# The four sums of tokens for the FFN's Strassen products by accumulating DMAs, with two quarters of the normed tokens kept negated

## The chip, the core and the metric

The kernel runs on one core of one Trainium2 chip. A core has five engines that run their own queues in order: TensorE (PE) multiplies, VectorE (DVE), ScalarE (ACT) and GpSimd (POOL) work elementwise, and SyncE (SP) issues most DMAs. GpSimd can issue DMAs as well, from its own queue. All DMAs run on the core's 16 DMA engines. The metric is the device time of one execution in microseconds (us), as the median of several runs.

## What is computed

The reference is one step of a two-layer recurrent decoder over 512 prompt tokens and 8 x 8 sample tokens, 576 in all, with 1024 channels. Each layer mixes tokens, adds a projection to `x`, and then applies the feed-forward network (FFN) that the change is about:

```
def _rmsnorm(x, w):
    xf = x.astype(jnp.float32)
    y = xf * lax.rsqrt(jnp.mean(xf * xf, axis=-1, keepdims=True) + NORM_EPS)
    return (y * w.astype(jnp.float32)).astype(x.dtype)
...
    x = x + y.astype(x.dtype)
    h = _rmsnorm(x, lw['ffn_norm'])
    g, u = jnp.split(h @ lw['w_ffn_in'], 2, axis=-1)
    x = x + ((jax.nn.silu(g) * u) @ lw['w_ffn_out']).astype(x.dtype)
```

`g` and `u` have 2816 columns each, which the kernel takes as 22 column blocks of 128.

## The kernel before

Channels lie on the 128 partitions: `x[k]` is a tile of 128 channels by 576 tokens, k from 0 to 7, and a *half* is 288 tokens. Every product in half precision is made of three matmuls: an fp32 operand is split into a high part (a cast, on ScalarE) and a low part (what the cast lost, on VectorE or GpSimd), and hi x hi, hi x lo and lo x hi are added up in PSUM.

`out_proj` adds the mixer's projection to `x`, sums squares for the norm, and starts the norm of half 0 (`norm_half` with `keep`). `norm_tiles` writes the normed value over `x[k]`, casts it to the high part of `h[k]` on ScalarE (L464) and makes the low part (L465) on VectorE, for some k on GpSimd.

`ffn` then works off the first three of the 22 blocks as plain GEMMs, `up(m, w, half)`: blocks 0 to 2 of half 0, then blocks 0 to 2 of half 1. Each fills two PSUM buffers (`fb`) of a ring of four; they come free when `gated` has read them with `fsg` on ScalarE and `fy` on VectorE. While they run, the norm of half 1 is made, and `strassen_tokens` makes four sums of quarters of the normed tokens. A quarter is four channel tiles of one half: b11 (k 0 to 3, half 0), b12 (k 0 to 3, half 1), b21 (k 4 to 7, half 0) and b22 (k 4 to 7, half 1). The sums overwrite the quarters, and `split` makes the 32 parts `st0` to `st3` of them.

Blocks 3 to 21 use Strassen's scheme in Winograd's form: 7 products instead of 8 for a 2 x 2 arrangement of (g, u) x (half 0, half 1). `strassen_weights` prepares the weights' seven operands of a block (`hA..`, `hS..`) with one accumulating DMA (L1709), three GpSimd additions (L1707) and seven splits on ScalarE (L1703) and VectorE (L1704). The preparation of block m+1 runs beside the products of block m. The order on each engine's queue is written out by a scheduler when the kernel is built; at run time each queue is worked off strictly in that order, and an operation that waits for a semaphore holds back all behind it.

Of the kernel before, what the change touches and what calls it, by code (L numbers as in the profile page):

```python
# [10 lines left out]
F32 = mybir.dt.float32  # L11
F16 = mybir.dt.float16
I32 = mybir.dt.int32
AF = mybir.ActivationFunctionType
ALU = mybir.AluOpType
PSUM = bass.MemoryType.PSUM
ADD, SUB, MUL, MAX, MIN = ALU.add, ALU.subtract, ALU.mult, ALU.max, ALU.min
# [6 lines left out]
DEPTH = 2  # L24
DFF = 2816
KT = D // 128
# [24 lines left out]
PBASE = {}  # L51
# [123 lines left out]
class Net:  # L175
# [159 lines left out]
    def setup(self):  # L335

        nc, t, cp = self.nc, self.io, self.cp
        rows = self.wp.tile([128, GW], F32, tag="raw", name="prow")[:, :128]
        for n, k in PARAMS:
            b = PBASE[n][0]  # L340
# [14 lines left out]
        for i, a in enumerate(self.x0):  # L355
            k, hs = 2 * (i % 4), slice(HW * (i // 4), HW * (i // 4) + HW)
# [13 lines left out]
        nc.tensor.transpose(ps, rows[:NPAR, :], self.ident[:NPAR, :NPAR])  # L370
        nc.vector.tensor_copy(self.pc[:, 2 * KT:], ps[:, 2 * KT:])
        nc.vector.tensor_scalar(self.pc[:, 2 * KT:4 * KT], self.pc[:, 2 * KT:4 * KT], HS, None, op0=MUL)
        for n in ("rw_w0", "rw_a0"):
            b, k = PBASE[n]
            nc.vector.tensor_scalar(self.pc[:, b:b + 2 * k], self.pc[:, b:b + 2 * k], 0.5, None, op0=MUL)
        b = PBASE["rw_kk"][0]
        nc.vector.tensor_scalar(self.pc[:, b:b + 4], self.pc[:, b:b + 4], 2.0 ** 15, None, op0=MUL)
        b = PBASE["rw_ka"][0]
# [3 lines left out]
        b = PBASE["hg_lb_logits"][0]  # L382
# [74 lines left out]
    def norm_tiles(self, name, l, half, r, x, keep):  # L457
        nc = self.nc
        hs = slice(half * HW, half * HW + HW)
        for k in range(KT):  # L460
            o = x[k] if keep else self.t("e", [128, HW], "nrm")
            hi, lo = self.h[k][:, 0, hs], self.h[k][:, 1, hs]
            nc.vector.scalar_tensor_tensor(o, x[k], self.par(name, l, k), r, op0=MUL, op1=MUL)
            nc.scalar.copy(hi, o)  # L464
            (nc.gpsimd if k % 3 == 2 or l == half == 0 and k % 2 else nc.vector).tensor_tensor(lo, o, hi, op=SUB)  # L465
# [1157 lines left out]
    def mix(self, l, prepared):  # L1623
# [3 lines left out]
        for half in range(2):  # L1627
            for i in range(3):
                for _ in range(2):
                    next(units[i])  # L1630
                if half == 0 and i == 0:
                    if l:
                        self.norm_half("attn_norm_w", l, 1)
                    else:
                        self.first_norm(1)
                        setup = self.setup()
                        next(setup)
                if l == 0 and half == 1 and i == 0:
                    run(setup)
# [37 lines left out]
    def strassen_tokens(self):  # L1677

        nc = self.nc
        out = [self.t("gd", [128, 4, 2, HW], f"st{i}", F16) for i in range(4)]  # L1680
        h0, h1 = slice(0, HW), slice(HW, T)
        src = []
        for k in range(4):
            b11, b12, b21, b22 = (self.x[k + o][:, h] for o in (0, 4) for h in (h0, h1))
            for i, (dst, a, b) in enumerate(((b11, b12, b11), (b12, b22, b12), (b22, b22, b11), (b21, b21, b22))):
                nc.gpsimd.tensor_tensor(dst, a, b, op=SUB)
                src.append(((0, 2, 1, 3)[i], k, dst))
        yield out
        for i in (3, 1, 0, 2):
            for j, k, dst in src:  # L1690
                if i == j:
                    self.split(out[i][:, k, 0], out[i][:, k, 1], dst)
            yield out

    def strassen_weights(self, key, load, ring, **rings):
# [258 lines left out]
```

## Time and profile before

| what | value |
|---|---|
| median of 3 runs | 2200.59 us (2200.28 to 2201.81) |
| the profiled execution | 2207.72 us |
| its span, first to last instruction | 2205.9 us |
| TensorE, VectorE, ScalarE, GpSimd busy | 92%, 74%, 49%, 31% |
| mean granted TensorE clock | 0.977 of full speed |
| sums of tokens, layer 0 | from 735.50 us |
| first Strassen matmul, layer 0 | 765.84 us |

Times in the rows are in us from the start of the span, unless marked ns. In a timeline each row has its start, its length (for several operations merged into a row, from the first's start to the last's end), the engine, the source line, the operation, `written<-read`, the shape and the count; in brackets stands how long the engine idled before it, and for whom. In the rows by line, the busy time and the mean length in ns follow the first bar. The rows of a window have its length, then for each engine the busy time and the number of instructions in the order TensorE, its weight loads, VectorE, ScalarE, GpSimd, and then the granted clock, the busy share of the DMA engines and GB/s.

### The profile page before, as it was taken

How to read it: one execution, taken by the hardware profiler on the slowest of the kernel's cores; microseconds unless marked ns; L12 is line 12 of the kernel's file. 1: busy time of each engine (PE TensorE's matmuls, PEld its weight loads, DVE VectorE, ACT ScalarE, POOL GpSimd, SP SyncE). 2: the span in 40 equal slices, each digit the busy share in tenths (PEclk: the TensorE clock that was granted, in tenths of full speed). 3: DMA queues.
4: the chain of work that ended last, by engine and by line, in shares of the span. 5: the costliest groups of instructions: out<-in, count | busy, mean ns of one | idle time of the engine just before them, and what ended most of it. 6: DMA issues, size and time to landing. Idle time of an engine off the chain costs nothing.

```text
span 2205.9 us, 42236 instructions
## 1 busy us (share of the span) xinstructions
PE 2039.1 (92%) x15754; PEld 1612.3 (73%) x15754; DVE 1636.6 (74%) x3409; ACT 1081.3 (49%) x2524; POOL 682.3 (31%) x889
## 2 busy tenths in 40 slices
PE   7989999998888899999999889989998988999998
PEld 5767787786676677777777778768776766777776
DVE  7889667768785899863488986586788779998441
ACT  6554546345444555442466355453645465554332
POOL 2223222146550544320012142213465316443000
PEclk9999999999999999999999999999999999999999
DMA  6312224333435344343421222242343443443331
GB/s 181 84 41 62 58 58 110 77 83 92 116 98 177 80 116 120 87 135 103 122 68 46 58 62 60 73 111 62 87 120 88 131 141 97 111 116 87 121 106 51
DMA packets 373498, 209.59 MB, mean 95 GB/s; under 512 B 59810, under 2 KB 360410, under 8 KB 373292
## 3 DMA queue, kind: packets, MB, share of 16 engines
q1 hardware_dynamic: 365516, 192.73, 31.6%
q0 software_dynamic: 7776, 14.16, 3.6%
q8 instruction: 124, 2.03, 0.4%
q14 instruction: 82, 0.67, 0.1%
HBM read 173.72 MB, written 16.59 MB: 86 GB/s over the span
## 4 chain that ended last, share of the span: by engine, by line
PE 47%; DVE 28%; ACT 8%; issue 7%; DMA 5%; POOL 3%; SPq 1%; DVEq 0%; ACTq 0%; POOLq 0%
PE pb L243 5%; PE pb L242 5%; PE pb L241 5%; PE xb L243 4%; PE xb L242 4%; PE xb L241 4%; DVE hA L1704 4%; DVE hS L1704 3%; DVE sc L1745 2%; DVE fy L1776 2%; DVE whl L229 2%; DVE su L1745 2%; PE fsS L1731 2%; PE fsS L1729 2%; PE fsS L1730 2%
## 5 line engine op out<-in xcount | busy, mean ns | idle before, releaser
L241 PE MATMUL pb<-h,whl 128*128 128x288 f16 (+1 forms) x1504 | 435.8, 290 | 4.4 <-ACT h L464 2.2
L243 PE MATMUL pb<-h,whl 128*128 128x288 f16 (+1 forms) x1504 | 435.5, 290 | 3.2 <-DVE whl L229 3.1
L242 PE MATMUL pb<-h,whl 128*128 128x288 f16 (+1 forms) x1504 | 436.0, 290 | 0.6 <-DVE h L465 0.4
L229 DVE SCALAR_TENSOR_TENSOR whl<-raw,whl 128x512 f16<-128x512 f32 (+1 forms) x352 | 253.8, 730 | 134.3 <-ACT whl L228 132.2
L242 PEld LDWEIGHTS <-whl 128*128 128x128 f16 (+1 forms) x2784 | 275.4, 99 | 88.0 <-issue 13.5
L243 PEld LDWEIGHTS <-whl 128*128 128x128 f16 (+1 forms) x2784 | 275.1, 99 | 88.0 <-issue 12.7
L241 PEld LDWEIGHTS <-whl 128*128 128x128 f16 (+1 forms) x2784 | 277.2, 100 | 76.6 <-issue 3.6
L228 ACT ACTIVATE whl<-raw 128x512 f16<-128x512 f32 (+1 forms) x352 | 213.3, 618 | 168.2 <-PE pb L243 51.9
L243 PE MATMUL xb<-fa,whl 128*128 128x288 f16 x704 | 201.3, 286 | 0.0
L242 PE MATMUL xb<-fa,whl 128*128 128x288 f16 x704 | 201.3, 286 | 0.0
L241 PE MATMUL xb<-fa,whl 128*128 128x288 f16 x704 | 201.3, 286 | 0.0
L1729 PE MATMUL fsA<-h,hA 128*128 128x288 f16 x432 | 124.3, 288 | 14.9 <-DVE gu L1550 10.8
L1729 PE MATMUL fsS<-st,hS 128*128 128x288 f16 x456 | 132.6, 291 | 5.9 <-ACT hS L1703 5.9
L1731 PE MATMUL fsS<-st,hS 128*128 128x288 f16 x456 | 132.4, 290 | 0.4 <-DVE hS L1704 0.3
L1730 PE MATMUL fsS<-st,hS 128*128 128x288 f16 x456 | 132.5, 291 | 0.0
L1731 PE MATMUL fsA<-h,hA 128*128 128x288 f16 x432 | 124.2, 288 | 1.7 <-DVE hA L1704 1.6
L1730 PE MATMUL fsA<-h,hA 128*128 128x288 f16 x432 | 124.3, 288 | 0.0
L1707 POOL TENSOR_TENSOR raw<-raw 128x512 f32<-128x512 f32 x52 | 79.0, 1520 | 134.2 <-DVE hA L1704 129.7
L1729 PEld LDWEIGHTS <-hS 128*128 128x128 f16 x864 | 85.7, 99 | 35.9 <-ACT hS L1703 13.7
L1704 DVE SCALAR_TENSOR_TENSOR hA<-sraw,hA 128x512 f16<-128x512 f32 x110 | 103.1, 945 | 10.6 <-ACT hA L1703 10.6
L1707 POOL TENSOR_TENSOR sraw<-sraw 128x512 f32<-128x512 f32 x60 | 89.7, 1499 | 51.4 <-DVE hA L1704 45.7
L1731 PEld LDWEIGHTS <-hS 128*128 128x128 f16 x864 | 85.7, 99 | 24.8 <-DVE hS L1704 2.6
(486 smaller groups left out, 5257.8 us busy)
## 6 DMA issues: line engine op xcount, KB each, us to landing
raw<-in_w_in SPq DMA_DIRECT2D x208, 256.0 KB
sraw<-in_w_ffn_in SPq DMA_DIRECT2D x40, 512.0 KB
raw<-in_w_ffn_out SPq DMA_DIRECT2D x80, 256.0 KB
raw<-in_w_ffn_in SPq DMA_DIRECT2D x78, 256.0 KB
x<-xd SPq DMA_DIRECT2D x32, 288.0 KB
raw<-sraw POOLq DMA_DIRECT2D x34, 256.0 KB, 3.3
sraw<-in_w_in SPq DMA_DIRECT2D x32, 256.0 KB
raw<-in_w_out SPq DMA_DIRECT2D x32, 256.0 KB
```

The lines of the kernel that those rows point to most:

```text
L228: nc.scalar.activation(hl[:, 0, :n], raw[:, :n], AF.Copy, scale=WS)
L229: nc.vector.scalar_tensor_tensor(hl[:, 1, :n], raw[:, :n], WS, hl[:, 0, :n], op0=MUL, op1=SUB)
L241: nc.tensor.matmul(ps, wh, hi, start=i == 0, stop=False)
L242: nc.tensor.matmul(ps, wh, lo, start=False, stop=False)
L243: nc.tensor.matmul(ps, wl, hi, start=False, stop=i == len(ks) - 1)
L1704: nc.vector.scalar_tensor_tensor(hl[:, 1], a, WS, hl[:, 0], op0=MUL, op1=SUB)
L1707: nc.gpsimd.tensor_tensor(dst, a, b, op=op)
L1729: nc.tensor.matmul(ps, w[a][:, 0, k], hi, start=k == 0, stop=False)
L1730: nc.tensor.matmul(ps, w[a][:, 0, k], lo, start=False, stop=False)
L1731: nc.tensor.matmul(ps, w[a][:, 1, k], hi, start=False, stop=k == 3)
L1745: nc.vector.tensor_tensor(o, a, p, op=ADD)
L1776: nc.vector.scalar_tensor_tensor(y, u, PH * AS, sg, op0=MUL, op1=MUL)
```

## The change

The 16 subtractions on GpSimd (four sums, four tiles each, 128 x 288 in fp32) become 16 DMAs that GpSimd issues and that add one SBUF tile onto another. [...] Two of the four sums, `st0` and `st3`, come out with the other sign, which `split` turns. GpSimd keeps the low parts of odd k among the quarters that are not negated.

```
@@ setup
+        b, k = PBASE["ffn_norm_w"]
+        self.npc = cp.tile([128, DEPTH * k], F32, name="npc")
+        nc.vector.tensor_scalar(self.npc, self.pc[:, b:b + DEPTH * k], -1.0, None, op0=MUL)
@@ norm_tiles
             hi, lo = self.h[k][:, 0, hs], self.h[k][:, 1, hs]
+            if keep:
+
+                neg = (k < 4) == (half == 1)
+                w = self.npc[:, KT * l + k:KT * l + k + 1] if neg else self.par(name, l, k)
+                nc.vector.scalar_tensor_tensor(o, x[k], w, r, op0=MUL, op1=MUL)
+                nc.scalar.activation(hi, o, AF.Copy, scale=-1.0 if neg else 1.0)
+                if neg:
+                    nc.vector.scalar_tensor_tensor(lo, o, -1.0, hi, op0=MUL, op1=SUB)
+                else:
+                    (nc.gpsimd if k % 2 else nc.vector).tensor_tensor(lo, o, hi, op=SUB)
+                continue
@@ strassen_tokens
-        for k in range(4):
-            b11, b12, b21, b22 = (self.x[k + o][:, h] for o in (0, 4) for h in (h0, h1))
-            for i, (dst, a, b) in enumerate(((b11, b12, b11), (b12, b22, b12), (b22, b22, b11), (b21, b21, b22))):
-                nc.gpsimd.tensor_tensor(dst, a, b, op=SUB)
-                src.append(((0, 2, 1, 3)[i], k, dst))
+        b11, b12, b21, b22 = ([self.x[k + o][:, h] for k in range(4)] for o in (0, 4) for h in (h0, h1))
+
+        for j, dst, a in ((0, b11, b12), (2, b12, b22), (1, b22, b11), (3, b21, b22)):
+            for k in range(4):
+                nc.gpsimd.dma_start(out=dst[k], in_=a[k], accum_op=ADD)
+                src.append((j, k, dst[k]))
         yield out
         for i in (3, 1, 0, 2):
             for j, k, dst in src:
                 if i == j:
-                    self.split(out[i][:, k, 0], out[i][:, k, 1], dst)
+                    self.split(out[i][:, k, 0], out[i][:, k, 1], dst, -1.0 if i in (0, 3) else 1.0)
             yield out
```

Line numbers of the changed kernel are higher by 3 to 15 behind these edits: L465 is now L473 and L475, L1686 is L1701, L1703 is L1718, L1707 is L1722, L1709 is L1724 and L1774 is L1789.

GpSimd's queue in layer 0 from the DMA ahead of the sums on, before (`x0` to `x7` are the tiles of `x`, each named for both halves; `h2` and `h5` are low parts of half 1):

```order
L1709 DMA sraw_9671<-sraw_9671 128x512
L1686 TENSOR_TENSOR x0_8557<-x0_8557 128x288
...
L1686 TENSOR_TENSOR x0_8557<-x4_8843,x0_8557 128x288
L465 TENSOR_TENSOR h2_9099<-x2_8699,h2_9099 128x288
...
L465 TENSOR_TENSOR h5_9102<-x5_8854,h5_9102 128x288
...
L1686 TENSOR_TENSOR x7_8876<-x7_8876,x3_8771 128x288
L1686 TENSOR_TENSOR x7_8876<-x7_8876 128x288
L1709 DMA raw_9338<-sraw_9340 128x512
L1707 TENSOR_TENSOR raw_9334<-raw_9338,raw_9334 128x512
```

And the same stretch of the changed kernel:

```order
L1724 DMA sraw_9673<-sraw_9673 128x512
L1701 DMA x0_8559<-x0_8559 128x288
...
L1701 DMA x1_8629<-x5_8856 128x288
L475 TENSOR_TENSOR h5_9104<-x5_8856,h5_9104 128x288
...
L1701 DMA x3_8773<-x7_8878 128x288
L475 TENSOR_TENSOR h7_9106<-x7_8878,h7_9106 128x288
L1701 DMA x4_8845<-x0_8559 128x288
...
L1701 DMA x7_8878<-x7_8878 128x288
L1724 DMA raw_9340<-sraw_9342 128x512
L1722 TENSOR_TENSOR raw_9336<-raw_9340,raw_9336 128x512
```

The sums are now made kind by kind instead of tile by tile, and the `h` parts left to GpSimd are h5, behind six of the DMAs, and h7, behind eight.

ScalarE's queue behind the casts of half 1, before (`fa` is a block's activation, `fsg` its gate read from PSUM, `st` the splits of the sums, `hA11` the first operand of the next weights):

```order
L464 CAST h7_9104<-x7_8876 128x288
L248 ACTIVATE st3_9317<-x4_8843 128x288
L248 ACTIVATE st3_9317<-x5_8854 128x288
L248 ACTIVATE fa1_9392<-fy_9395 128x288
L248 ACTIVATE st3_9317<-x6_8865 128x288
L248 ACTIVATE st1_9315<-x4_8843 128x288
L1774 ACTIVATE fsg_9450<-fb_9399 128x288
L248 ACTIVATE st3_9317<-x7_8876 128x288
...
L1703 ACTIVATE hA11_9757<-raw_9334 128x512
L1774 ACTIVATE fsg_9506<-fb_9456 128x288
```

And in the changed kernel:

```order
L471 ACTIVATE h7_9106<-x7_8878 128x288
L248 ACTIVATE fa1_9394<-fy_9397 128x288
L1789 ACTIVATE fsg_9452<-fb_9401 128x288
L248 ACTIVATE fa2_9451<-fy_9454 128x288
L248 ACTIVATE st3_9319<-x4_8845 128x288
...
L248 ACTIVATE st3_9319<-x7_8878 128x288
L248 ACTIVATE st1_9317<-x6_8867 128x288
L1789 ACTIVATE fsg_9508<-fb_9458 128x288
...
L1718 ACTIVATE hA11_9759<-raw_9336 128x512
L248 ACTIVATE fa0_9280<-fy_9510 128x288
```

The gate and the activations of half 0's blocks 1 and 2 have moved ahead of the splits, and the gate of half 1's block 0 stands behind seven of them; of those, the splits of `st3` wait for the last of the four sums. VectorE's queue has the same turn with `fy` and the low parts.

## Rows read from the trace of the kernel before

**Rows 1.** From the page: busy us, share of span and instructions of TensorE.

```profile
PE 2039.1 (92%) x15754; PEld 1612.3 (73%) x15754; DVE 1636.6 (74%) x3409; ACT 1081.3 (49%) x2524; POOL 682.3 (31%) x889
```

**Rows 2.** Windows: a stretch of the Strassen blocks of layer 0.

```profile
800.00:850.00 50.00, 47.84 (x389) 37.80 (x387) 49.87 (x81) 26.72 (x57) 23.66 (x19) 1.00 0.47 124
```

**Rows 3.** Chain of waits, 733 to 770 us: start, length, what, times.

```profile
740.47 0.91 POOL h L465
...
751.61 0.90 POOL x L1686
752.53 3.57 ACT st L248 x11
...
758.25 0.61 DVE hA L1704
...
765.84 0.28 PE fsA L1729
```

**Rows 4.** Chain of waits, 1815 to 1855 us (layer 1).

```profile
1834.28 0.90 POOL x L1686
```

**Rows 5.** Timeline of GpSimd, 640 to 800 us.

```profile
734.89 0.88 POOL L1709 DMA_DIRECT2D sraw<-sraw  x1 [7.75 <-DVE x L463]
735.50 2.60 POOL L1686 TENSOR_TENSOR x<-x 128x288 f32<-128x288 f32 x3
...
752.44 0.88 POOL L1709 DMA_DIRECT2D raw<-sraw  x1
```

**Rows 6.** Instructions of L463 and L465: ns min/median/max, first and last start.

```profile
L463 DVE SCALAR_TENSOR_TENSOR x<-x,pc,rstd x32: 505/518/3372, 713.5 to 1826.2; 128x288 f32<-128x288 f32 x32
...
L465 DVE TENSOR_TENSOR h<-x,h x21: 444/453/1046, 714.8 to 1828.5; 128x288 f16<-128x288 f32 x21
```

**Rows 7.** Waits of TensorE, 733 to 770 us: total, times, longest.

```profile
PE fb L242 <- DVE h L465: 4.2, 4, 2.6
PE fb L241 <- ACT fsg L1774: 2.1, 1, 2.1
PE fb L241 <- DVE fy L1776: 1.1, 1, 1.1
PE fsA L1729 <- ACT fsg L1774: 0.8, 1, 0.8
```

**Rows 8.** Accumulating DMA: GpSimd by line, two windows, issue with us to landing.

```profile
L1709 POOL DMA_DIRECT2D raw<-sraw x34 | 30.0, 883 | 70.5 <-DVE fy L1776 44.5 <-DVE hA L1704 15.9 <-DVE su L1745 6.7
...
734.90:736.30 1.40, 1.40 (x14) 1.10 (x13) 1.40 (x2) 1.39 (x3) 1.40 (x3) 1.00 0.00 0
736.30:737.80 1.50, 1.50 (x15) 1.20 (x13) 1.50 (x1) 0.51 (x2) 1.50 (x3) 1.00 0.96 175
...
sraw<-sraw POOLq DMA_DIRECT2D x1, 256.0 KB, 3.3
```

**Rows 9.** Loads: SyncE's timeline from 740 us; the page's hardware queue (packets, MB, share).

```profile
743.15 7.12 SPq L1798 DMA_DIRECT2D sraw<-in_w_ffn_in  x4
...
q1 hardware_dynamic: 365516, 192.73, 31.6%
```

**Rows 10.** DMA issues, 1955 to 1968 us: KB each, us to landing.

```profile
sraw<-sraw POOLq DMA_DIRECT2D x1, 256.0 KB, 3.2
raw<-sraw POOLq DMA_DIRECT2D x1, 256.0 KB, 4.9
```

**Rows 11.** Timeline of VectorE, 700 to 800 us.

```profile
713.55 1.38 DVE L463 SCALAR_TENSOR_TENSOR x<-x,pc,rstd 128x288 f32<-128x288 f32 x3 [3.65 <-ACT rstd L445]
...
715.21 3.23 DVE L463 SCALAR_TENSOR_TENSOR x<-x,pc,rstd 128x288 f32<-128x288 f32 x4
...
745.79 0.68 DVE L465 TENSOR_TENSOR h<-x,h 128x288 f16<-128x288 f32 x1
...
753.01 2.67 DVE L250 TENSOR_TENSOR st<-x,st 128x288 f16<-128x288 f32 x7 [0.20 <-ACT st L248]
...
758.17 0.69 DVE L1704 SCALAR_TENSOR_TENSOR hA<-raw,hA 128x512 f16<-128x512 f32 x1
```

## The prediction, made before the changed kernel ran

> **What bounds the kernel now.** I read the page first. TensorE holds 92% of the span [rows 1], so whatever the change touches off TensorE counts only where TensorE, or the engine that feeds it, waits. Next I read the windows of the Strassen blocks: from 800 to 850 us VectorE is busy 49.87 of 50.00 us and TensorE 47.84 [rows 2]. VectorE sets the pace there, so a Strassen stage that starts late ends late by as much, and one that starts early ends early by as much.
>
> Then I asked what releases that stage. The chain of waits around its start runs almost without a break through the work that the change replaces: VectorE's norms, GpSimd's `h` and `x` operations until 751.61 + 0.90, ScalarE's splits of the token sums from 752.53, VectorE's first `hA` of the next weights at 758.25, and TensorE's first Strassen matmul at 765.84 [rows 3]. In layer 1 the last `x` operation starts at 1834.28 [rows 4], 1082.7 us after that of layer 0, and the steps behind it repeat, so I work out layer 0 and double it.
>
> In GpSimd's timeline the sums begin at 735.50, behind a DMA issue at 734.89, with two `h` parts among them; the next DMA issue comes at 752.44 [rows 5]. So 16 subtractions and two `h` parts take 735.50 to 752.51, 17.0 us. Two things besides happen in that time. VectorE's norm multiply, 0.518 us in the median, goes up to 3.372, and its `h` subtraction from 0.453 up to 1.046 [rows 6]: the two engines hold each other up. And TensorE waits 4.2 us for `h`, 2.1 for `fsg` and 1.1 for `fy` [rows 7].
>
> **The change, part by part, for one layer.** The sum's question is when the last token sum is there: 752.51 before; after, when the sixteenth DMA lands.
>
> *Start.* The DMA at 734.89 stays and takes 0.88 us [rows 5, 8]. The first sum's DMA can be issued at 735.77.
>
> *Issue.* GpSimd's cost of one DMA is 0.88 us [rows 8], for 128 rows of 2 KB; ours has 128 rows of 1152 B. The next operation begins 0.61 us after a DMA's start [rows 5], so one issue costs between 0.61 and 0.88. I take 0.84, near the full duration: an operation recorded as started may still wait for the one ahead, and no row shows two such DMAs in a row. The two `h` parts left in the queue (now h5 and h7) cost 0.91 each in the chain [rows 3]; I count 0.85, with less of VectorE in the way. The sixteenth issue then starts at 735.77 + 15 x 0.84 + 2 x 0.85 = 750.1.
>
> *Transfer.* The trace has the accumulating DMA on 256 KB alone. Its engines stand still until 1.4 us after the issue, are 0.96 busy for the next 1.50 (so 1.44 us), and it has landed 3.3 after the issue [rows 8]: 1.45 + 1.44 + 0.36. For 144 KB, 144/256 of 1.44 gives 0.81. The bound from below is the plain hardware queue: 192.73 MB in 31.6% of 2205.9 us is 3.6 us per MB [rows 9], 0.53 us for 147 KB; no row shows an accumulating transfer that fast, so I take 0.83 (rows shorter by half keep their fixed part). The sixteenth lands at 750.1 + 1.45 + 0.83 + 0.36 = 752.7 if nothing else moves.
>
> *Dependencies.* A b12 sum waits until the b11 sum of its tile has landed, a b22 sum for the b12 one, a b21 sum for the b22 one. Four issues lie between a sum and the one that needs it, 4 x 0.84 = 3.4 us against 1.45 + 0.83 + 0.36 = 2.6 to landing. The waits are covered as long as landing stays under 3.4, and not when issues come at 0.61.
>
> *Other transfers.* The same engines load weights: four `sraw` loads are issued between 743.15 and 750.27 [rows 9]. TensorE's progress releases them, so they fall into the sums' time after too. 256 KB is 0.26 x 3.6 = 0.9 us each, 3.7 us in all. The sums alone fill the engines for 16 x 0.83 = 13.3 us from 737.2. That loads do delay an accumulating DMA is seen where they overlap: one lands after 4.9 us instead of 3.2 [rows 10]. With none of the loads in the way the end is 752.7, with all of it 750.5 + 3.7 + 0.36 = 754.6; I count 0.7 of it, and since a delayed landing also delays the issues that wait for it, I take 754.0.
>
> *Behind the last sum.* VectorE has 13 operations left before `hA`, each 0.37 us after the one ahead (7 in 2.67 [rows 11]), 4.8 us; ScalarE's split ahead of the first, one of those that come 11 in 3.57 [rows 3], with its hand-overs is some 0.6. That makes 5.4 us, against 758.17 - 752.51 = 5.7 before [rows 11]. So `hA` starts at 754.0 + 5.4 = 759.4, 1.2 us late. From `hA` on, the GpSimd additions, the `hS` splits and the evacuations that free PSUM for the blocks stand as before. TensorE's last wait of 0.8 ahead of the first block [rows 7] gives back some 0.2, since its other work is then long done. That is +1.0 us a layer.
>
> *What is freed, and why it does not pay.* VectorE's operations return to 0.45 and 0.52 us: about 8 us of its time, between 735 and 747. TensorE's waits for `h`, 4.2 us, shrink to about 2: the h7 part stands in GpSimd's queue behind eight DMAs, at 735.77 + 8 x 0.84 + 0.85 = 743.3, and ends at 744.2, where the last `h` came at 745.79 + 0.68 = 746.47 [rows 11]. The waits of 2.1 and 1.1 go, since `fsg` and `fa` now stand ahead of the splits. TensorE reaches the end of its six GEMMs some 5 us earlier, and waits there, because `fsg` of the next pair stands behind the `hS` that needs GpSimd's addition, which needs `hA`. VectorE idles from about 741 until the first b21 sum lands.
>
> *The rest.* The `npc` multiply (128 x 16, once, in the setup) and ScalarE's cast that becomes an activation of the same shape cost nothing that I count. In layer 0 VectorE takes over three of GpSimd's five `h` parts of the first half, 3 x 0.45 = 1.3 us more. Against it, four norm multiplies there take 3.23 us where three took 1.38 just before [rows 11], 1.4 us over their pace, which GpSimd's five parts caused. The two even out; without that cover the half-1 norms would be 1.3 us late, once.
>
> **Sum.** 2 x 1.0 = +2.0 us. The profiled execution took 2207.72 us (span 2205.9 and 1.8 around it), 7.1 over the median of 2200.59; I add the difference to the median: 2202.6, that is 0.1%. A measurement here tells 0.2% or 4.4 us from no change.
>
> **Pages against rows.** The stretched 3.372 and 1.046 us of VectorE show in the rows that two engines exclude each other [rows 6]. The Trainium skill, SBUF — State Buffer, Who interferes with whom, says that a VectorE instruction with two SBUF inputs contends with a GpSimd instruction that reads SBUF, by a lock held for the whole instruction; by this rule the lock goes away with the change, and the trace agrees so far. If VectorE were the path, the page's rule would give the first rival. The Trainium skill, DMA: Bandwidth & Descriptors, Anatomy of one DMA, puts a DMA at 2.0 us plus bytes over 436 GB/s, 2.3 us for ours as an estimate; by it the sums would be bound by issue alone and the last would land at 752.4, a gain of 0.4 us a layer. The row at 3.3 us for 256 KB, where the page gives 2.6, speaks against it.
>
> **Rivals.**
> *VectorE is the path (faster).* If the splits were not held in queue order behind the last sum, TensorE's 4.2 + 2.1 + 1.1 us a layer [rows 7] would be won: 2200.6 - 14.8 = 2185.8. The order of ScalarE's queue speaks against it. 0.05.
> *The DMAs are quick (faster).* Issue at 0.61, transfer at 0.53, loads in the gaps: the sixteenth issue starts at 747, landing at 749.8, `hA` at 755.2, 2.9 us early, 2194.8. It decides from a landing before 750.8. For it: the 0.61 that the row shows; against it: the engine time of 1.44 us per 256 KB. 0.13.
> *The transfers are the bound (slower).* All 3.7 us of loads, 0.87 a transfer, and landings over 3.4 us that stop GpSimd at its in-order waits: the last lands at 756, `hA` at 761.4, 3.2 late less the 0.2, 2206.6. It decides from a landing after 755.2. For it: 0.96 busy engines and the 4.9 us; against it: most landings alone take 3.2 to 3.3. Behind GpSimd's waiting DMA stand h7, which TensorE waits for, and the next weights' DMA and additions. 0.32 with its tail.
> *No change that can be measured:* the forecast. 0.50.
>
> **The numbers.** Faster by over 0.2% 0.18, within 0.2% 0.50, slower 0.32. The bounds of issue, transfer and loads give landings of 749.5 to 756.5, -6.6 to +7 us; leaving out the first rival and the last of the slow tail, the range is 2195 to 2209.
>
> **What would show it.** Right: 32 DMA issues of `x` near 0.84 us apart on GpSimd; VectorE's norms of the second half at 0.5 us; the last sum landing near 754 and the first `hA` near 759.4; TensorE's wait for `h` halved and a longer wait ahead of the first Strassen matmul. Wrong: issues 0.6 us apart, landings under 2.4 us, or a Strassen stage that no longer starts with this `hA`.

## The result, and the profile after

The changed kernel takes 2214.09 us (median of 4 runs, 2213.85 to 2214.68) against 2201.2 before (4 runs, 2200.28 to 2203.31): ratio 1.006, interval 1.0048 to 1.0072. A second series gave 2217.58 against 2204.58, ratio 1.0056 (1.0044 to 1.0068). It is slower by 12 to 13 us, where the forecast was 2.0 and the range ended at 2209, 8 us above the median of before.

The page of the changed kernel, to be read beside [rows 1] and the queues: TensorE does the same instructions, VectorE is busy for 18 us less, and the software queue's transfers take 5.2% of the span.

```profile
PE 2045.4 (92%) x15754; PEld 1616.8 (73%) x15754; DVE 1618.4 (73%) x3413; ACT 1079.0 (49%) x2524; POOL 679.1 (31%) x886
...
q0 software_dynamic: 12384, 18.88, 5.2%
```

VectorE's timeline of the changed kernel in layer 0. What [rows 6] showed as up to 3.372 us is gone: norms go at 0.5 us, and the longest takes 0.992. Then VectorE stands idle for 13.62 us.

```profile
731.19 1.38 DVE L470 SCALAR_TENSOR_TENSOR x<-x,npc,rstd 128x288 f32<-128x288 f32 x3 [1.30 <-ACT rstd L448]
...
733.28 1.37 DVE L470 SCALAR_TENSOR_TENSOR x<-x,pc,rstd 128x288 f32<-128x288 f32 x3
...
753.22 0.46 DVE L252 SCALAR_TENSOR_TENSOR st<-x,st 128x288 f16<-128x288 f32 x1 [13.62 <-ACT st L248]
```

GpSimd's timeline of the same stretch, which answers to [rows 5]. The sixteen DMAs and two `h` parts run from 734.60 to 751.92 + 0.86 = 752.78, 18.2 us, where sixteen subtractions and two `h` parts took 17.0.

```profile
734.60 3.84 POOL L1701 DMA_DIRECT2D x<-x  x4
739.02 1.75 POOL L1701 DMA_DIRECT2D x<-x  x2 [0.58 <-DVE fy L1791]
...
743.40 1.05 POOL L475 TENSOR_TENSOR h<-x,h 128x288 f16<-128x288 f32 x1
744.08 4.77 POOL L1701 DMA_DIRECT2D x<-x  x5
749.43 1.75 POOL L1701 DMA_DIRECT2D x<-x  x2 [0.58 <-DMA x<-x]
751.92 0.86 POOL L1701 DMA_DIRECT2D x<-x  x1 [0.74 <-DMA x<-x]
752.51 1.16 POOL L1724 DMA_DIRECT2D raw<-sraw  x1
```

The chain of waits of the changed kernel, which answers to [rows 3]. Where VectorE and GpSimd stood, landings now stand (`DMA x<-x`), and the last sum is there at 751.92 + 4.60 = 756.52. From there to the first `hA` of the next weights, 762.12, it is 5.6 us.

```profile
735.67 5.18 DMA x<-x
...
744.67 4.48 DMA x<-x
...
749.43 1.75 POOL x L1701 x2
...
751.92 4.60 DMA x<-x
...
758.44 1.47 DVE st L252 x4
...
762.12 0.61 DVE hA L1719
...
762.86 2.20 POOL raw L1722
...
770.84 0.31 PE fsA L1744
```

The DMA queues of the changed kernel from 732.69 to 757.19, 24.5 us (packets, MB, share of the 16 engines). With 78.6% and 15.7% the engines are all but full from the first sum to the last (one window, 744 to 746 us, has a share of 0.65). The stretch holds the sixteen sums and two DMAs of 256 KB, at 1.44 us each [rows 8]: (0.786 x 24.5 - 2 x 1.44) / 16 = 1.02 us a sum. This is time of packets: from 736.30 to 756.50 us the shares add up to 1.09, so packets overlap on the engines, and spread over them a sum takes some 1.02 / 1.09 = 0.94 us (an estimate). The weights' loads take 0.157 x 24.5 = 3.8 us.

```profile
q0 software_dynamic: 2589, 2.88, 78.6%
q1 hardware_dynamic: 2122, 1.05, 15.7%
```

All instructions of the sums' line in the changed kernel: a DMA lands 4.5 us after its start in the median.

```profile
L1701 POOL DMA_DIRECT2D x<-x x32: 859/1184/2237, 734.6 to 1839.3; - x32
...
DMA to landing us min/median/max: 3.0/4.5/6.0
```

TensorE's waits from 728 to 775 us in the changed kernel, to be read beside [rows 7]. The wait for `h` has not halved (in the profile of the second series it is 3.6), and 5.0 us of waits now stand at the first Strassen products: 1.9 ahead of the first matmul, 3.1 behind its first twelve.

```profile
PE fb L242 <- POOL h L475: 5.3, 2, 3.3
PE fsA L1744 <- DVE fy L1791: 3.1, 1, 3.1
PE fsA L1744 <- ACT fsg L1789: 1.9, 1, 1.9
```

In TensorE's timeline the first Strassen matmul is the one at 766.06; the row of 770.84 in the chain above is the thirteenth.

```profile
766.06 0.28 PE L1744 MATMUL fsA<-h,hA 128*128 128x288 f16 x1 [1.89 <-ACT fsg L1789]
...
770.84 0.31 PE L1744 MATMUL fsA<-h,hA 128*128 128x288 f16 x1 [3.15 <-DVE fy L1791]
```

Where is the time lost? The stage ends with the first matmul of the output GEMM (`xb`). In the kernel before that is 972.89 - 733.45 = 239.44 us behind the first norm of half 1, in the changed one 976.69 - 731.19 = 245.50 (timelines of VectorE and TensorE).

```profile
733.45 1.38 DVE L463 SCALAR_TENSOR_TENSOR x<-x,pc,rstd 128x288 f32<-128x288 f32 x3 [1.30 <-ACT rstd L445]
...
972.89 0.29 PE L241 MATMUL xb<-fa,whl 128*128 128x288 f16 x1
```

```profile
976.69 0.29 PE L241 MATMUL xb<-fa,whl 128*128 128x288 f16 x1
```

The same points read from the traces of these kernels, counted from the first norm of half 1, mean of both layers (and of two profiles for the first two rows), in us:

| kernel | last sum there | first hA | first xb | ratio to before |
|---|---|---|---|---|
| before | 19.1 | 24.7 | 240.2 | 1 |
| changed | 24.5 | 30.0 | 246.0 | 1.0056 |
| 72 KB a sum (e_half) | 21.6 | 27.1 | 243.7 | 1.0050 |
| 18 KB a sum (e_tiny) | 21.2 | 27.0 | 242.9 | 1.0026 |
| no chain (e_nochain) | 23.1 | 25.8 | 241.7 | 1.0027 |
| splits as sums land (e_order) | 24.5 | 16.2 | 242.3 | 1.0018 |
| `h` on VectorE (e_hdve) | 24.2 | 29.0 | 244.7 | 1.0040 |
| GpSimd additions (e_gpadd) | 19.6 | 25.6 | 242.2 | 1.0029 |
| half by DMA, half VectorE (e_mix) | 15.2 | 21.8 | 237.7 | 0.9983 |
| VectorE additions (e_dve) | 12.7 | 21.3 | 236.6 | 0.9976 |
| before, sums on VectorE (b_dve) | 13.1 | 21.1 | 235.0 | 0.9959 |

The change costs 5.8 us a layer in this stage, 11.6 in all, and 5.3 of the 5.8 are there at the first `hA`. The spans of these profiles differ by 10.1 us in the mean (2212.4 and 2218.2 against 2205.9 and 2204.5) and not by 11.6, mostly because in layer 0 the first norm of half 1 comes 1.3 us sooner; the medians differ by 12 to 13.

### The profile page after: what moved, and what is told of

It reads as the page before. It is cut to its first block, busy times and chain, and to the rows that moved or that the text cites. A ratio compares the mean times of both kernels' runs of the same rounds, so it can differ in the third digit from the quotient of the medians.

```text
span 2212.4 us, 42268 instructions
## 1 busy us (share of the span) xinstructions
PE 2045.4 (92%) x15754; PEld 1616.8 (73%) x15754; DVE 1618.4 (73%) x3413; ACT 1079.0 (49%) x2524; POOL 679.1 (31%) x886
## 4 chain that ended last, share of the span: by engine, by line
PE 49%; DVE 29%; issue 7%; ACT 7%; DMA 5%; POOL 2%; SPq 0%; DVEq 0%; POOLq 0%; ACTq 0%
PE pb L243 5%; PE pb L242 5%; PE pb L241 5%; PE xb L243 4%; PE xb L242 4%; PE xb L241 4%; DVE hA L1719 3%; DVE hS L1719 3%; DVE sc L1760 2%; DVE fy L1791 2%; DVE whl L229 2%; DVE su L1760 2%; PE fsS L1746 2%; PE fsS L1744 2%; PE fsS L1745 2%
## 5 line engine op out<-in xcount | busy, mean ns | idle before, releaser
L243 PEld LDWEIGHTS <-whl 128*128 128x128 f16 (+1 forms) x2784 | 275.5, 99 | 86.7 <-issue 11.6
L1744 PE MATMUL fsA<-h,hA 128*128 128x288 f16 x432 | 125.1, 290 | 21.7 <-DVE gu L1564 9.1
L1722 POOL TENSOR_TENSOR raw<-raw 128x512 f32<-128x512 f32 x52 | 79.1, 1521 | 140.2 <-DVE hA L1719 135.7
L1719 DVE SCALAR_TENSOR_TENSOR hA<-sraw,hA 128x512 f16<-128x512 f32 x110 | 99.6, 914 | 11.8 <-ACT hA L1718 11.8
L1722 POOL TENSOR_TENSOR sraw<-sraw 128x512 f32<-128x512 f32 x60 | 90.0, 1504 | 54.2 <-DVE hA L1719 52.4
```

The source lines that it names most:

```text
L243: nc.tensor.matmul(ps, wl, hi, start=False, stop=i == len(ks) - 1)
L1719: nc.vector.scalar_tensor_tensor(hl[:, 1], a, WS, hl[:, 0], op0=MUL, op1=SUB)
L1722: nc.gpsimd.tensor_tensor(dst, a, b, op=op)
L1744: nc.tensor.matmul(ps, w[a][:, 0, k], hi, start=k == 0, stop=False)
```

## The experiments

**The two kernels again.** The kernel before, unchanged:

> The kernel before, unchanged, profiled once more. Its first profile is an execution of 2207.72 us, 6.5 over the median of the others. If that is chance: about 2201 us, and the two traces differ at a few places by 6.5 us together, which tells how much of the 6.3 us between the two profiles belongs to the change and how much more the change costs beside it. If the profiler itself costs 6.5 us for this kernel: about 2207.5 again.

It took 2206.25 us, by this number alone nearer to the second reading. But the 26 runs of before in its series spread from 2197.35 to 2209.64 with a median of 2204.42, and the profiled executions of other kernels lie on either side of their medians (e_dve 2195.95 against 2199.49, e_order 2209.82 against 2209.15). So the first profile, 2207.72, was more likely an execution from the upper part of a spread than the profiler's price. Its stage takes the same: 19.0 to 19.1 to the last sum in both profiles and layers.

> The changed kernel itself, timed beside more runs of the kernel before, whose runs now spread from 2197 to 2210 us with a median of 2204.4. If the 12.9 us are right: 2214 against 2204, ratio 1.004 to 1.006. If the kernel before only had a good series: the changed kernel spreads as widely, and its ratio falls towards the 1.003 that the two profiles show.

2217.58 against 2204.58: the loss stands, and both kernels move by some us from series to series.

**Additions in place of the DMAs**, on GpSimd (e_gpadd) and on VectorE (e_dve). The quarters b12 and b21 are normed with the negated weights `npc` here as in the changed kernel, so that an addition makes the difference:

```
-                nc.gpsimd.dma_start(out=dst[k], in_=a[k], accum_op=ADD)
+                nc.gpsimd.tensor_tensor(dst[k], dst[k], a[k], op=ADD)   # e_gpadd
+                nc.vector.tensor_tensor(dst[k], dst[k], a[k], op=ADD)   # e_dve
```

> Negated norms and signs of the changed kernel, but each sum by a GpSimd addition in place of an accumulating DMA. Theory 'transfers' (the cost is the DMA engines, full from the first sum to the last): the loss goes, 2198 to 2203, with the last sum done at about 15.5 to 17.5 us after the first one starts. Rival 'negation' (VectorE's part of the change costs): stays near 2210 or over.

2211.09, ratio 1.0029 (1.0019 to 1.0039): the time lies where the rival "negation" had it. The last sum is there at 19.6, 17.0 behind the start of the first, as the theory had it; so the DMAs' lateness is gone, but a loss of half the size is not (2.0 of the 5.8 us a layer at `xb`). Its chain of waits points to another cause than the negated norms: the order of the sums puts the last `h` part at 749.16, 16.8 behind the first norm of half 1, and TensorE starts behind it. In the kernel before it stood at 745.79, 12.3 behind. This was not tried by itself, so negation is not ruled out.

```profile
749.16 0.91 POOL h L475
...
750.12 0.40 PE fb L242
```

The additions on GpSimd also bring the stretched norms back, up to 4.475 us where the DMAs left 0.992 and additions on VectorE 0.994. So it is GpSimd's arithmetic that holds VectorE up, as the prediction read [rows 6].

```profile
L470 DVE SCALAR_TENSOR_TENSOR x<-x,pc,rstd x16: 504/518/4475, 712.4 to 1830.0; 128x288 f32<-128x288 f32 x16
```

> As the one with GpSimd additions, but the sixteen additions are VectorE's. VectorE idles 13.6 us behind its norms in the changed kernel. Theory 'transfers': 16 x about 0.45 us, the last sum some 7.5 us behind the last norm, near 747 on the scale of the changed kernel, so the first hA some 6 us earlier than before and 9 earlier than in the changed kernel; GpSimd and VectorE no longer hold each other up: 2201 - 2 x 5 = about 2191. Rival 'the stage is bound elsewhere' (TensorE's GEMMs or fsg ahead of it): within 3 us of before.

2199.49, ratio 0.9976 (0.9966 to 0.9985): 4.9 us under the kernel before of its series, between the two expectations. The sums are there 6 us earlier than before and `hA` 3.4; 3.6 a layer arrive at `xb`. It fell short of the 5 expected: from the last sum to `hA` it is now 8.7 us and not 5.6, with VectorE at the splits, and TensorE waits 5.0 us for `fsg`.

**No sum waits for another**, first try: each DMA adds a constant tile.

```
-                nc.gpsimd.dma_start(out=dst[k], in_=a[k], accum_op=ADD)
+                nc.gpsimd.dma_start(out=dst[k], in_=self.cst[:, :HW], accum_op=ADD)
```

> The sixteen accumulating DMAs as in the changed kernel, but each adds the same constant tile, so that none waits for another sum (the sums are not those of the reference; this prices the chain). Theory 'transfers': the engines stay full, the last one lands within 1 us of 756.5 counted on the changed kernel's scale (22 us behind the first issue), 2211 to 2215 us. Rival 'chain' (GpSimd's queue waits for landings): issues come 0.6 to 0.9 apart without gaps, the last lands 3 to 5 us earlier, 2203 to 2208.

2203.51, ratio 0.9998 (0.9986 to 1.001). The time lies in the rival's range, but it tells nothing apart: with a source that is there from the start, eight of the sixteen DMAs went out before the norms of half 1, so it took away the chain and half of the crowd at once.

**No sum waits for another**, second try, with the constant tile held back until the first norm of half 1:

```
+                if half and not k:
+                    nc.vector.scalar_tensor_tensor(self.cst[:, :1], o[:, :1], 0.0, self.cst[:, :1], op0=MUL, op1=ADD)
```

> The sixteen accumulating DMAs at the place, in the order and of the size of the changed kernel, but each adds one constant tile, which a 128 x 1 operation of VectorE behind the first norm of the second half holds back until then. No sum reads another sum, so the waits for a landing four issues back go (the sums are not the reference's). The changed kernel: 24.5 us from the first norm of the second half to the last landing, hA at 30.0; with an eighth of the bytes 19.5 to 22.9, hA 25.7 to 28.4. Theory 'full engines': the waits only pass on what the engines do anyway, last landing 23 to 25, hA 28.5 to 30.5, ratio 1.004 to 1.006. Rival 'chain': GpSimd issues in 16.0 us without a gap, last landing 21 to 22, hA 26.5 to 27.5, ratio 1.002 to 1.0035.

2209.63, ratio 1.0027 (1.0016 to 1.0039). GpSimd's timeline has no gap: the issues end at 744.10 + 8.61 = 752.71, 16.2 us behind the first one at 736.53.

```profile
736.53 6.51 POOL L1703 DMA_DIRECT2D x<-cst  x7
...
744.10 8.61 POOL L1703 DMA_DIRECT2D x<-cst  x6
749.87 3.73 POOL L1726 DMA_DIRECT2D raw<-sraw  x1
```

The last DMA lands at 756.62, 20.1 us behind the first issue, where it was 21.9 (756.52 - 734.60). So the chain is worth 1.8 us to the last landing; the rest of the lateness stays, with the engines as full as in the changed kernel (76.9% and 16.0% of 24.5 us). Landings are later than ever (here from a recorded start that lies up to 4.5 us ahead of the end of the issue), though no issue waits. The sums' line:

```profile
DMA to landing us min/median/max: 3.7/6.4/7.7
```

By the first `hA` it gains 4.2, more than by the landing, because the queue did not keep the order of the changed kernel: the scheduler put the first sum of `st3` sixth of the sixteen, where it stood thirteenth, and ScalarE's splits start at 745.56. Both theories have their part; the ratio fell where the rival put it, for this second reason as well, and does not price the chain alone.

**Fewer bytes**: the DMAs over half of the columns (e_half) and, with HW // 8, one eighth (e_tiny).

```
-                nc.gpsimd.dma_start(out=dst[k], in_=a[k], accum_op=ADD)
+                nc.gpsimd.dma_start(out=dst[k][:, :HW // 2], in_=a[k][:, :HW // 2], accum_op=ADD)
```

> The changed kernel with accumulating DMAs over half of the columns, 72 KB each in place of 144 (the other half of each sum is left out, so the products are not the reference's). Issues, waits and the order stay. Theory 'transfers' (engines full from 736 to 756.5 us): the engines' work falls by 16 x 0.5 = 8 us, the last sum lands near 748 to 749 and a layer gains 7 to 8 us: 2198 to 2203. Rival 'chain' (fixed time to landing, and GpSimd waiting for it in its queue): a landing is 0.5 us shorter, 4 levels of it, 2 us a layer: 2209 to 2211.

2216.78, ratio 1.005 (1.0036 to 1.0065): both expectations missed. By the table the stage gains 2.3 us a layer, not 7 to 8 and near the rival's 2; of these 4.6 us in all the medians show 0.8, with six runs from 2210.26 to 2220.15. I had overlooked that with fewer bytes GpSimd's issues become the bound: here they end 16.2 us behind the first one.

> The changed kernel with accumulating DMAs over one eighth of the columns, 18 KB each (the rest of each sum is left out, the products are not the reference's). From the first norm of the second half to the last landing it was 24.5 us with 144 KB and 21.6 with 72 KB; to the first hA 30.0 and 27.1. Theory 'issue floor' (sixteen issues of 0.89 us and two h parts of 0.9 on GpSimd, 16.0 us, and 2 us to land): 20.5 to the last landing, 26.0 to hA, still 1.3 behind the kernel before (24.7): 2205 to 2212. Rival 'bytes alone' (2.9 us a half, going on): 19.4 to the last landing, 24.9 to hA, 2202 to 2206.

2207.67, ratio 1.0026 (1.0017 to 1.0035), as the issue floor has it. GpSimd's timeline of e_tiny: sixteen issues and two `h` parts from 732.07 to 740.32 + 7.76 = 748.08, 16.0 us without a wait for a landing.

```profile
732.07 5.63 POOL L1701 DMA_DIRECT2D x<-x  x6
736.90 1.61 POOL L475 TENSOR_TENSOR h<-x,h 128x288 f16<-128x288 f32 x1
737.58 2.67 POOL L1701 DMA_DIRECT2D x<-x  x2
739.64 1.36 POOL L475 TENSOR_TENSOR h<-x,h 128x288 f16<-128x288 f32 x1
740.32 7.76 POOL L1701 DMA_DIRECT2D x<-x  x8
```

Its landings, of all instructions of the line:

```profile
DMA to landing us min/median/max: 2.5/3.1/5.5
```

So even with almost nothing to move the sums come 2 us later than GpSimd's own subtractions. The issue of one DMA costs 0.89 us there, the subtraction that it replaces 0.95 in the mean ((17.0 - 2 x 0.91) / 16).

**The splits in the order in which sums land**, in the changed kernel (e_order), and tile by tile in the kernel before (b_order):

```
-        for i in (3, 1, 0, 2):
+        for i in (0, 2, 1, 3):
```

> The changed kernel, but the sixteen splits stand in ScalarE's and VectorE's queues in the order in which the sums land (b11, b12, b22, b21) and not with the last one first. Theory 'the last landing plus what is held behind it': the last sum still lands near 756.5, twelve of the sixteen splits are done by then, hA comes some 3 us earlier: 2 x 3 = 6 us, 2207 to 2209. Rival 'only the landing counts, the engines behind it keep up': no change, 2213 to 2215.

2209.15, ratio 1.0018 (1.0009 to 1.0026), 8.4 us below the changed kernel of the same series. The last sum lands as late as ever (24.5), but twelve splits and the first `hA` no longer stand behind it.

> The kernel before, with its own GpSimd subtractions, and the splits in the order of the sums, tile by tile (a control for the split order, which gave the changed kernel 8.4 us back). If splits held behind the last sum cost the kernel before as much: hA some 3.5 us earlier, 2197 to 2199. If its last sum is too near the end for that: 2203 to 2206.

2200.97 against 2200.62, ratio 1.0001 (0.9993 to 1.001). Before the change the order cost nothing; what the DMAs made late, the order held up.

**The `h` parts of odd k on VectorE**, in the changed kernel:

```
-                    (nc.gpsimd if k % 2 else nc.vector).tensor_tensor(lo, o, hi, op=SUB)
+                    nc.vector.tensor_tensor(lo, o, hi, op=SUB)
```

> The changed kernel with the last h parts (h5 and h7 of the second half, two more in the first half) on VectorE in place of GpSimd. TensorE waited 5.3 us for h there, and its granted clock fell to half for the 6 us behind it. Theory 'transfers': that wait lies beside the transfers and is not on the path; GpSimd issues its DMAs 2 us earlier, but the engines are full: the last landing stays within 0.7 us of 756.5, 2212 to 2215. Rival 'TensorE's wait and its clock': 4 us a layer back, 2205 to 2207.

2214.21, ratio 1.004 (1.0028 to 1.0052), as the first theory has it. TensorE's wait for `h` is gone, and a wait of 8.2 us for `fsg` stands in its place (its waits, 728 to 775 us):

```profile
PE fb L241 <- ACT fsg L1789: 8.2, 1, 8.2
PE fsA L1744 <- DVE fy L1791: 2.7, 1, 2.7
```

The first DMA starts 1.1 us behind the first norm, where it was 2.2 to 3.4 (the scheduler put three of the sums ahead of the weights' DMA), and two operations fewer stand in GpSimd's queue; but the queue stops for 5.9 us at landings (728 to 775 us), and the last sum lands at 24.2. What the issues save goes into waits.

```profile
POOL x L1701 <- DMA x<-x: 5.9, 4, 2.3
```

**Half of the sums by DMA**: b11 and b12 by DMA, b22 and b21 on VectorE.

```
+                if j in (0, 2):
                     nc.gpsimd.dma_start(out=dst[k], in_=a[k], accum_op=ADD)
+                else:
+                    nc.vector.tensor_tensor(dst[k], dst[k], a[k], op=ADD)
```

> The changed kernel with eight of the sums (b11, b12) as accumulating DMAs and eight (b22, b21) as VectorE additions. By the issue floor the eighth DMA is issued about 2.4 + 7 x 0.89 + 1.8 = 10.4 us behind the first norm and lands 3 to 4 later, 14; VectorE's additions, 0.37 us each, go beside the landings and end near 16; hA some 6 behind, 22: about as with all sixteen on VectorE (hA 21.3), ratio 0.997 to 0.999. Rival 'any DMA in the chain costs' : the landings come 4.5 us behind the issues, hA 25 and later, ratio 1.000 to 1.003.

2201.66, ratio 0.9983 (0.9974 to 0.9992), as expected: the sums are there at 15.2, `hA` at 21.8. Eight DMAs still keep VectorE waiting for 5.09 us (its timeline):

```profile
749.87 0.46 DVE L1704 TENSOR_TENSOR x<-x,x 128x288 f32<-128x288 f32 x1 [5.09 <-DMA x<-x]
```

**All sums on VectorE**: with the splits reordered as well (e_dve_order), and in the kernel before, without negation (b_dve).

```
-                nc.gpsimd.tensor_tensor(dst, a, b, op=SUB)
+                nc.vector.tensor_tensor(dst, a, b, op=SUB)   # b_dve
```

> The sums as VectorE additions (2199.5 against 2204.4 before) and the splits in the order of the sums in place of last one first. Theory 'the time of the first hA on VectorE sets the layer's end': ScalarE's splits run beside the additions, the last split is done some 17 us behind the first norm in place of 21.3, 2 x 4 less: 2190 to 2193. Rival 'TensorE's GEMMs set it' (they end 30 us behind the first norm, no earlier than before): 2197 to 2201.

2196.35 against 2200.62, ratio 0.9976 (0.9967 to 0.9986), that of e_dve: the order gains nothing, as the rival has it. The first `hA` stays at 21.7. In layer 0 ScalarE's last split starts 13.0 behind the first norm, where it was 17.8 in e_dve, but VectorE's at 21.7, where it was 20.9: VectorE has the additions and its half of the splits to do.

> The kernel before with its sixteen subtractions on VectorE in place of GpSimd, no negation. Theory 'the lateness of the sums is what counts, negation nothing': like the additions on VectorE, 2197 to 2201. Rival 'the negated norms pay': 2203 to 2206.

2191.55, ratio 0.9959 (0.9945 to 0.9974): the fastest, 9 us below the kernel before of its series and below both expectations. VectorE's timeline shows sums 0.37 us apart (two from 739.78 to 740.52), less than half of what GpSimd or an issue takes, and the first `hA` at 750.23, 21.2 behind the first norm at 728.99.

```profile
728.99 1.38 DVE L463 SCALAR_TENSOR_TENSOR x<-x,pc,rstd 128x288 f32<-128x288 f32 x3 [1.30 <-ACT rstd L445]
...
739.78 0.81 DVE L1686 TENSOR_TENSOR x<-x,x 128x288 f32<-128x288 f32 x2
740.52 0.45 DVE L1686 TENSOR_TENSOR x<-x 128x288 f32<-128x288 f32 x1
...
750.23 0.68 DVE L1704 SCALAR_TENSOR_TENSOR hA<-raw,hA 128x512 f16<-128x512 f32 x1
```

## Why the prediction was wrong

**What bounds the kernel** was read rightly: `hA` late by 5.3 us is `xb` late by 5.8, and in most kernels of the table the two move together. In e_order they part, since there the first `hA` goes ahead of splits that are still to come. The first Strassen matmul, which the prediction named too, is a poor mark: it comes only 1.7 us later than before, and twelve matmuls on TensorE waits for VectorE.

**The step that failed is "Dependencies"**: "the waits are covered as long as landing stays under 3.4", with 2.6 us to a landing, taken from a DMA that had the engines to itself. Landings take 4.5 us in the median, and 4.60 for the last sum, whose issue had no other ahead of it; so GpSimd's queue stops at DMAs that need a tile of a sum which has not landed. Of its four pauses in layer 0 (0.58, 0.48, 0.58 and 0.74 us) the trace names a landing for the last two; the first two end 0.6 us behind the landings of the first and the fourth sum (738.41 and 742.22), whose tiles the next DMA needs. Counted from the first issue, the forecast had the last landing at 754.0 - 735.77 = 18.2 us; layer 0 has 21.9. The 3.7 us between:
- *Issue, +0.8.* I had the issues done 750.1 + 0.84 - 735.77 = 15.2 behind the first. Without any wait it takes 16.0 (e_tiny): 0.89 each and not 0.84. The full 0.88 of [rows 8] was the right reading.
- *Waits for landings, +2.2.* In the changed kernel the issues take 18.2, against 16.0 in e_tiny. e_nochain, where no sum waits for another, takes 16.2.
- *The tail, +0.7.* From the end of the last issue to its landing 756.52 - 752.78 = 3.7 us, forecast 3.1.

Behind the waits and the tail stand the terms "Transfer" (0.83 us forecast; 1.02 of packet time, some 0.94 spread over the engines, which makes 16 x 0.11 = 1.8 us a layer) and "Other transfers" (0.7 of the loads' time counted, all of it, 3.8, inside the stretch). Together they fill the engines, and the chain passes the fullness on to GpSimd. So the terms are not to be added: without the chain (e_nochain) 1.8 of the 3.7 go, and 1.9 stay, 1.0 of them in the issues and the rest in the tail.

**Behind the last sum** 5.4 was forecast and 5.6 came. The sum's error is all ahead of it: +1.2 forecast at `hA`, +5.3 measured as mean of layers and profiles, of which the later start of the first DMA, 3.4 us behind the first norm in one of four cases and 2.2 to 2.7 in the others, is a part of 0.3.

**What is freed** on VectorE came and did not pay, as forecast: the norms run at 0.5 us and VectorE idles. TensorE's part did not come. The h7 part was forecast to end 744.2 - 733.45 = 10.8 behind the first norm and ended 13.3 behind it (11.8 to 13.3 in the four cases); TensorE's wait for `h` was 5.3 and 3.6 us and not 2. Nor did TensorE reach the end of its six GEMMs 5 us earlier: its last `fb` matmul starts 32.7 us behind the first norm, where it was 31.3 (layer 0), with the granted clock at 0.50 for 6 us in between. e_hdve shows that the wait for `h` lies beside the DMAs and hardly counts.

**The rivals.** "The transfers are the bound" was the mechanism, mis-sized: it had the last landing at 756 on the scale of before, 22.6 behind the first norm, and it is 24.5. Two figures do not follow from the prediction's own terms, without weight here: the quick rival's landing adds up to 747 + 1.45 + 0.53 + 0.36 = 749.3 and not 749.8, and the bound of +7 us ends at 2207.6 and not at 2209. That VectorE is the path was wrong for this kernel, but the time that VectorE idles can be used: on VectorE the sums gain what the DMAs lose.

**Pages against rows.** A DMA here lands 4.5 us after its start, with the engines full, and 3.1 even with 18 KB. The Trainium skill, DMA: Bandwidth & Descriptors, Anatomy of one DMA, with 2.0 us and bytes over 436 GB/s gives 2.3 for 144 KB as an estimate and calls the making of descriptors small. The trace agrees with neither: even the 256 KB that had the engines to themselves took 3.3 us [rows 8], and each DMA costs 0.89 us of GpSimd's time. GpSimd's record of the last sum ends at 752.78 and its landing is 756.52: the Trainium skill, Perfetto Trace Analysis, DMA Instruction — SWDGE (GPSIMD), says that this end is that of descriptor making and not of the data's way, and the trace agrees.

**What stays open.** Whether negated norms cost something by themselves: e_dve and b_dve differ by that, by the order of the sums and by the place of the `h` parts, 0.9976 against 0.9959, and their intervals overlap; and the 0.0029 that e_gpadd keeps is put down to the place of the last `h` part by its chain alone. How much of the loss the loads alone make was not tried; it is read from the queue's share only.

## What to carry to other kernels

An accumulating DMA is no free addition: here its issue took as much of GpSimd as the addition itself. Before such a move, add up the engine time of everything that lands in the stretch, and compare the landing under that load, not alone, with the distance between dependent issues. Ask first which engine idles behind the work: sixteen operations of 0.37 us a layer on VectorE gained 9 us in the kernel before, and 5 with the changed kernel's norms and order, where sixteen DMAs lost 12.

## What the runs showed of the hardware

The packet time of one accumulating DMA of 128 rows, as a share of the 16 engines, was 1.02 us with 144 KB, 0.62 with 72 and 0.35 with 18, worked out as above from the software queue's share of 24.5 us (78.6%, 52.1% and 34.4%). It does not fall in step with the bytes, with the 0.94 that is left of 1.02 without the overlap either. The shares of e_half and e_tiny:

```profile
q0 software_dynamic: 2592, 1.71, 52.1%
```

```profile
q0 software_dynamic: 2592, 0.82, 34.4%
```

Issues that stand in a row have recorded starts 0.5 to 0.6 us apart and growing lengths (1.18, 1.53, 1.89 and 2.24 us for the first four of the changed kernel); only their ends, 0.89 apart, tell the pace. And TensorE, which had waited for `h` with 5.3 us in all, had a granted clock of 0.50 from 744 to 750 us, the level of 1.2 GHz, while VectorE and ScalarE did nothing (windows of the changed kernel); from 752 to 756 it was back at 1.00.

```profile
744.00:746.00 2.00, 1.49 (x7) 0.95 (x7) 0.00 (x0) 0.00 (x0) 2.00 (x4) 0.50 0.65 89
746.00:748.00 2.00, 2.00 (x10) 1.26 (x9) 0.00 (x0) 0.00 (x0) 2.00 (x4) 0.50 1.11 205
748.00:750.00 2.00, 2.00 (x11) 1.23 (x9) 0.00 (x0) 0.00 (x0) 1.42 (x2) 0.50 1.18 185
```

It fell to 0.50 again from 771 to 774 us, behind the wait of 3.15 for `fy`. The clock does not explain the loss by itself: in b_dve, the fastest kernel, it fell to 0.50 as well, from 740 to 744 us, behind a stretch in which TensorE had been busy for 1.11 of 4 us.

```profile
740.00:744.00 4.00, 2.25 (x10) 1.45 (x10) 4.00 (x12) 4.00 (x14) 0.00 (x0) 0.50 0.36 66
```
